# First pair of feed-forward slabs by plain block products, and layer norms on VectorE, in a hybrid encoder layer

## The chip, the core and the metric

The kernel runs on one core of a Trainium2 chip. The metric is the device time of one execution in microseconds (us). The engines are named as in the profile: PE (TensorE, with PEld for its weight loads), DVE (VectorE), ACT (ScalarE), POOL (GpSimd) and SP (SyncE, which issues the DMAs).

## The reference, cut to what matters

One layer of an encoder with 1024 tokens of width 1024 in float32. Four layer norms end four sublayers; the first and third are half-step feed-forward layers with 2816 hidden columns:

```python
x = layer_norm(ALPHA * x + 0.5 * swiglu(x, ffn1_w1, ffn1_w3, ffn1_w2), ln1_g, ln1_b)
...                                   # attention and state-space mixers, w_out
x = layer_norm(ALPHA * x + merged @ w_out, ln2_g, ln2_b)
x = layer_norm(ALPHA * x + 0.5 * swiglu(x, ffn2_w1, ffn2_w3, ffn2_w2), ln3_g, ln3_b)
ple = sigmoid(x @ ple_w_gate) * (p @ ple_w_proj)
x = layer_norm(ALPHA * x + ple, ln4_g, ln4_b)

def swiglu(x, w1, w3, w2):
    return (silu(x @ w1) * (x @ w3)) @ w2
def layer_norm(x, g, b):              # over the 1024 columns
    return (x - mean) * rsqrt(var + 1e-5) * g + b
```

## The kernel before, in words

Every float32 factor is split into a high part that TensorE takes as it is and a low rest (`split`, L64 on ACT for the high part, L65 on DVE for the low one), and a product is three matmuls: high by high, high by low, low by high. A matmul has a 128x128 stationary block and 512 moving columns.

**The upward half of a feed-forward layer** (`ffn_up`) goes through 11 pairs of 128-column slabs of w1 and w3 (`NP` is 11; slab p goes with slab p + 11). For a pair, x and the two slabs are cut into two-by-two blocks (halves of the 1024 model rows, halves of the tokens for x, the two slabs for w), and the four block results come from 7 block products by a Strassen-Winograd scheme instead of 8. One block product is 12 matmuls (`prod`, L246), so a pair is 2 x 7 x 12 = 168 matmuls for w1 and w3. The seven factors of x (numbers 1 to 7 in `blocks_of`: xa holds 1 and 2, tb 6 and 5, tc 7 and 3, td 4) are made once: 1, 2 and 3 are blocks of x as they are, 4 to 7 need differences of blocks. The seven factors of w are made for each slab pair by `sums_of`. `product` adds up the block products in PSUM and SBUF, and after a pair four further combinations c1 and c2 of the result are made on POOL (L330 to L333) and written with the rest to `hd` in DRAM (L336), for the downward half (`ffn_down`, L405), which uses the same scheme.

**The first pair.** In the first layer x comes already transposed from DRAM (`rawx`, L482, four pairs of rows for each half of the tokens). `lead` loads the first slabs of w1 and w3, splits the first token half, runs block products 1 and 2 for both slabs (48 matmuls, L502), and then makes the differences of x: L511 and L513 on DVE, L520 and L521 on POOL, each followed by splits. The remaining 120 matmuls of the pair need the differences. In the second layer x comes from the second norm and is transposed by TensorE (`transpose_sums`, L170): token tiles 0 to 3 give factors 1 and 2, and for each of the tiles 4 to 7 the function turns tile j - 4 once more, copies it (L184), turns tile j, and makes all differences (L187, L188, L192 on DVE, L193 on POOL). `lead2` starts block products 1 and 2 and then calls `finish()`, which does tiles 4 to 7.

**A norm** (`layer_norm`, L118 to L140) of one tile of 128 tokens: the mean on DVE, the sum of squares on ACT (L121), eight operations on 128x1 columns, mostly on DVE (L122 to L128, L137), the square root on ACT (L123), then the tile itself: scaled and shifted on ACT (L138), times the gain on POOL (L139), plus the bias on DVE (L140). The last two tiles of the last norm take another way, two pairs of DVE operations on half a tile (L132, L134). The norms run as their tiles leave the matrix product before (`norm_in`): after a few tiles (`lag`) each step also transposes an earlier tile for the next product. In norms one, two and three the next product cannot start before tiles are normalised, transposed (L151, L170) and split.

**Order.** The program is written as a flow of tiles; a scheduler puts the instructions of each engine into one queue at compile time, by program order as priority and by a simulated time line. An engine works through its queue in that order. A tag with `bufs` is a set of buffers; a tile waits for one to come free. The tag "raw" (weight slabs before the split) has four, "uh" and "ul" (split slabs) three, "v" four, "a" eight, the PSUM tags "up" two and "dn" four.

Of the kernel before, what the change touches and what calls it, by code (L numbers as in the profile page):

```python
# [20 lines left out]
F32 = mybir.dt.float32  # L21
# [24 lines left out]
def layer_kernel(ctx, tc, A):  # L46
# [66 lines left out]
    def layer_norm(a, sums, gt, bt, pool, out=None):  # L113
# [15 lines left out]
        if out is not None:  # L129
            cs = [slice(c, c + 512) for c in (0, 512)]  # L130
            for c in cs:
                V.scalar_tensor_tensor(out=a[:, c], in0=a[:, c], scalar=nm, in1=gt[:, c], op0=ALU.add, op1=ALU.mult)  # L132
            for c in cs:
                V.scalar_tensor_tensor(out=a[:, c], in0=a[:, c], scalar=rs, in1=bt[:, c], op0=ALU.mult, op1=ALU.add)  # L134
                nc.sync.dma_start(out[:, c], a[:, c])
            return
# [25 lines left out]
    def transpose_sums(a, j, X, pool):  # L162

        (xa, tb, tc_, td), c = X, j % 4
        cs = slice(c * 128, c * 128 + 128)

        def turned(src):
            t = pup.tile([128, 1024], F32, tag="up", name="tln")
            for k in range(8):
                PE.transpose(t[:, k * 128:k * 128 + 128], src[:, k * 128:k * 128 + 128], idt)  # L170
            return t

        def k8(t):
            return t.rearrange("p (k n) -> p k n", n=128)

        if j < 4:
            t = turned(a[j])
            split(k8(t), xa[0][:, :, cs], xa[1][:, :, cs])
            return
        l, r = slice(0, 512), slice(512, 1024)  # L180
        t1 = turned(a[j - 4])
        pool = pool[0]
        o = pool.tile([128, 1024], F32, tag="v", bufs=4, name="xo")
        S.activation(o, t1, AF.Copy)  # L184
        t2 = turned(a[j])
        p = pool.tile([128, 1024], F32, tag="v", bufs=4, name="xp")
        V.tensor_tensor(out=p[:, r], in0=t2[:, l], in1=o[:, l], op=ALU.subtract)  # L187
        V.tensor_tensor(out=p[:, l], in0=t2[:, r], in1=p[:, r], op=ALU.subtract)  # L188
        split(k8(p), tb[0][:, :, cs], tb[1][:, :, cs])
        q = pool.tile([128, 1024], F32, tag="v", bufs=4, name="xq")  # L190
        S.activation(q[:, r], t2[:, r], AF.Copy)
        V.tensor_tensor(out=q[:, l], in0=q[:, r], in1=t2[:, l], op=ALU.subtract)  # L192
        G.tensor_tensor(out=o[:, l], in0=o[:, r], in1=p[:, l], op=ALU.subtract)  # L193
        split(k8(q), tc_[0][:, :, cs], tc_[1][:, :, cs])
        split(k8(o[:, l]), td[:, 0:4, cs], td[:, 4:8, cs])

    def norm_in(steps, acc, gt, bt, xT, pool, done=None, lag=3, sums_in=None):


        ready = []  # L200

        def bring(late):
            j = ready.pop(0)
            if sums_in:
                transpose_sums(acc, j, xT, sums_in)
            else:
                transpose_in(acc[j], j, xT, late)
            if done:
                done(j)

        def finish():
            while ready:
                bring(True)

        for j, sums in steps:
            layer_norm(acc[j], sums, gt, bt, pool)
            ready.append(j)
            if len(ready) > lag:
                bring(False)
        return finish  # L220
# [53 lines left out]
    def ffn_up(fp, X, w1, w3, hd, lead):  # L274
# [5 lines left out]

        def product(A, B, left, right, d21, begun=None):

            x, z = begun or start(A, B)
# [23 lines left out]
        for p in range(NP):  # L307
            begun = None, None
            if p == 0:
                rest, begun = lead(banks, start)  # L310
                A1 = rest[0]()
            else:
                A1 = sums_of(fp, *slabs_in(w1, p))
            s1, s2 = big("s1"), big("s2")
            product(A1, X, s1, s2, lambda x: S.activation(s2[:, l], x, AF.Silu), begun[0])
            S.activation(s1, s1, AF.Silu)
            S.activation(s2[:, r], s2[:, r], AF.Silu)
            A3 = rest[1]() if p == 0 else sums_of(fp, *slabs_in(w3, p))
# [5 lines left out]
            product(A3, X, e1, e2, times, begun[1])  # L324
# [3 lines left out]

            c1, c2 = big("c1"), big("c2")
            G.tensor_tensor(out=c1[:, l], in0=s1[:, r], in1=s2[:, r], op=ALU.add)  # L330
            G.tensor_tensor(out=c1[:, r], in0=c1[:, l], in1=s1[:, l], op=ALU.subtract)
            G.tensor_tensor(out=c2[:, l], in0=s1[:, l], in1=s1[:, r], op=ALU.subtract)
            G.tensor_tensor(out=c2[:, r], in0=s2[:, l], in1=c1[:, r], op=ALU.subtract)  # L333
            for i, t in ((1, s1[:, l]), (2, s2[:, l]), (4, s2[:, r]), (5, c1[:, l]), (6, c1[:, r]),
                         (7, c2[:, l]), (3, c2[:, r])):
                nc.sync.dma_start(hd[i - 1][p // 2][:, p % 2, :], t)  # L336
# [121 lines left out]
    with tc.tile_pool(name="f1", bufs=1, reuse_waits="tile") as fp:  # L458
# [6 lines left out]
        def lead(banks, start):  # L465
# [27 lines left out]
            B = blocks_of(xa, tb, tcs, td)  # L493
            bk = [banks() for _ in range(2)]
            for i, (x, y) in ((1, (0, 512)), (2, (512, 1024))):
                n = 0
                for k in range(4):
                    ks = slice(x + k * 128, x + k * 128 + 128)
                    for (o1, o2), (_, (wh, wl), _) in zip(bk, ws):
                        o = o1 if i == 1 else o2  # L500
                        for m, (u, v) in enumerate(((wh, 0), (wh, 1), (wl, 0))):
                            PE.matmul(o, lhsT=u[:, ks], rhs=B[i][v][:, k, :], start=(k == 0 and m == 0),  # L502
                                      stop=(k == 3 and m == 2), skip_group_check=True)
            for kp in range(2):
                bring(1, kp), bring(1, kp + 2)
            r2 = [load_raw(A[n][NP]) for n in ("ffn1_w1", "ffn1_w3")]
            t2s = []
            for kp in range(2):
                k = 2 * kp
                t1, b21, b12, b22 = raws[0][kp], raws[0][kp + 2], raws[1][kp], raws[1][kp + 2]  # L510
                V.tensor_tensor(out=t1, in0=b12, in1=t1, op=ALU.subtract)  # L511
                t2 = fp.tile([128, 2, 512], F32, tag="v", bufs=4, name="t2")
                V.tensor_tensor(out=t2, in0=b22, in1=t1, op=ALU.subtract)  # L513
                split(t2, tb[0][:, k:k + 2, :], tb[1][:, k:k + 2, :])
                t2s.append(t2)
            for kp in range(2):
                k = 2 * kp
                t1, b21, b12, b22 = raws[0][kp], raws[0][kp + 2], raws[1][kp], raws[1][kp + 2]
                split(t1, tb[0][:, k + 4:k + 6, :], tb[1][:, k + 4:k + 6, :])
# [897 lines left out]
```

## Time and profile before

| what | value |
|---|---|
| median of 3 runs | 2406.77 us (2405.56 to 2407.76) |
| the profiled execution's own time | 2407.14 us |
| its span in the profile | 2405.3 us |
| PE, DVE, ACT, POOL busy | 2273.2, 1625.7, 984.0, 623.6 us |
| granted clock of TensorE, mean | 0.974 |

The span runs from the first to the last instruction in the trace; the execution's own time is 1.8 us longer. In the timelines below a row gives the start in us, the duration in us, the engine, the line, the operation, its tiles and, in brackets, how long the engine had stood idle before it and what ended that.

### The profile page before, as it was taken

To read this page: it belongs to the slowest core of one execution; us is meant where nothing else is said; L and a number is where in the kernel's file an instruction comes from. 1 tells how busy PE (TensorE), PEld (TensorE's weight loads), DVE (VectorE), ACT (ScalarE), POOL (GpSimd) and SP (SyncE) were. 2 spreads that over 40 slices of the span, in tenths; PEclk is the share of its full clock that TensorE was granted. 3 is DMA by queue.
4 is the path that set the end of the run, shared out by engine and by line. 5 is a ranking of instruction groups with operands and counts; after the bars stand their busy time and mean duration, and the time that the engine had idled before them with its cause. 6 is when DMAs were issued, how large, how long until landed. Compare 5 with 4: busy or idle time off the path is not lost.

```text
span 2405.3 us, 28500 instructions
## 1 busy us (share of the span) xinstructions
PE 2273.2 (95%) x10704; PEld 1867.9 (78%) x10704; DVE 1625.7 (68%) x2316; ACT 984.0 (41%) x1390; POOL 623.6 (26%) x545
## 2 busy tenths in 40 slices
PE   5999999999979989998999999969999999999898
PEld 4888888877768878886888888758888888777686
DVE  7656565775587799948688875675656556764845
ACT  4333333333442313334477871353333333333627
POOL 2111010200038555524255542220201112000302
PEclk8999999999989989999999999979999999999899
DMA  3333232842244223335100034112323236622211
GB/s 122 113 97 120 84 114 86 316 184 95 81 143 144 94 75 90 105 127 214 62 10 27 27 129 160 40 57 93 122 88 119 88 110 255 239 94 95 75 53 70
DMA packets 103898, 265.62 MB, mean 110 GB/s; under 512 B 13264, under 2 KB 27856, under 8 KB 103760
## 3 DMA queue, kind: packets, MB, share of 16 engines
q1 hardware_dynamic: 103760, 263.80, 32.1%
q8 instruction: 84, 1.38, 0.2%
q14 instruction: 54, 0.44, 0.1%
HBM read 189.33 MB, written 74.42 MB: 110 GB/s over the span
## 4 chain that ended last, share of the span: by engine, by line
PE 76%; DVE 10%; issue 5%; DMA 4%; ACT 2%; POOL 1%; SPq 0%; DVEq 0%; ACTq 0%; POOLq 0%
PE px L246 19%; PE pg L84 11%; PE py L246 10%; PE pdy L405 7%; PE pd L405 7%; PE pz L246 5%; PE ps L84 3%; PE pd L84 2%; PE pov L693 2%; PE pya L84 2%; PE tpp L680 2%; DMA w2w<-in_ffn_w_dram 2%; PE pyb L84 2%; PE pq L84 1%; DVE acc L140 1%
## 5 line engine op out<-in xcount | busy, mean ns | idle before, releaser
L139 POOL TENSOR_TENSOR acc<-acc,ln 128x1024 f32<-128x1024 f32 x30 | 79.5, 2656 | 555.6 <-ACT acc L138 554.2
L330 POOL TENSOR_TENSOR c<-s,s 128x512 f32<-128x512 f32 x22 | 30.2, 1375 | 725.7 <-DVE s L325 654.4
L65 DVE TENSOR_TENSOR wlo<-raw,whi 128x1024 fp32r<-128x1024 f32 (+4 forms) x112 | 141.6, 1268 | 80.2 <-ACT whi L64 79.0
L64 ACT ACTIVATE whi<-raw 128x1024 fp32r<-128x1024 f32 (+4 forms) x112 | 107.6, 967 | 154.9 <-PE pg L84 111.7
L84 PE MATMUL pg<-xlo,whi 128*128 128x512 f32 x416 | 164.7, 396 | 0.3 <-DVE xlo L65 0.3
L84 PE MATMUL pg<-xhi,whi 128*128 128x512 f32 x416 | 164.8, 397 | 0.1
L84 PE MATMUL pg<-xhi,wlo 128*128 128x512 f32 x416 | 163.6, 393 | 0.0
L405 PE MATMUL pd<-wl,hh 128*128 128x512 f32 x352 | 144.0, 409 | 5.9 <-DVE wl L65 5.9
L405 PE MATMUL pd<-wh,hl 128*128 128x512 f32 x352 | 140.6, 403 | 0.0
L405 PE MATMUL pd<-wh,hh 128*128 128x512 f32 x352 | 125.3, 405 | 10.5 <-ACT hh L64 5.3
L64 ACT ACTIVATE wh<-w2w 128x1024 fp32r<-128x1024 f32 x56 | 59.3, 1058 | 166.3 <-PE pd L405 84.0
L246 PE MATMUL py<-tch,fhl 128*128 128x512 f32 x352 | 116.9, 392 | 0.0
L64 ACT ACTIVATE fhl<-raw 128x512 fp32r<-128x512 f32 x44 | 27.9, 633 | 202.3 <-PE px L246 197.2
L246 PE MATMUL px<-td,thi 128*128 128x512 f32 x352 | 108.8, 390 | 0.0
L65 DVE TENSOR_TENSOR hl<-raw,hh 128x1024 fp32r<-128x1024 f32 x84 | 101.3, 1208 | 10.2 <-ACT hh L64 8.2
L667 POOL TENSOR_SCALAR P<-P,sm 128x1024 f32<-128x1024 f32 x64 | 74.7, 1168 | 115.0 <-DVE sm L666 97.2
L260 DVE TENSOR_TENSOR c<-raw 128x512 f32<-128x512 f32 x44 | 37.8, 859 | 98.4 <-PE px L246 98.4
L405 PE MATMUL pdy<-wl,hh 128*128 128x512 f32 x264 | 104.3, 395 | 0.0
L405 PE MATMUL pdy<-wh,hl 128*128 128x512 f32 x264 | 103.9, 395 | 0.0
L405 PE MATMUL pdy<-wh,hh 128*128 128x512 f32 x264 | 99.7, 395 | 0.0
L65 DVE TENSOR_TENSOR wl<-w2w,wh 128x1024 fp32r<-128x1024 f32 x56 | 69.4, 1239 | 36.6 <-ACT wh L64 36.4
L65 DVE TENSOR_TENSOR pt<-tpp,pt 128x512 fp32r<-128x512 f32 x128 | 85.6, 684 | 11.6 <-ACT pt L64 10.1
(413 smaller groups left out, 6667.1 us busy)
## 6 DMA issues: line engine op xcount, KB each, us to landing
raw<-in_ffn_w_dram SPq DMA_DIRECT2D x86, 512.0 KB, 3.7
raw<-hd SPq DMA_DIRECT2D x70, 512.0 KB, 3.3
hd<-c SPq DMA_DIRECT2D x88, 256.0 KB, 4.4
hd<-s SPq DMA_DIRECT2D x66, 256.0 KB, 2.9
w2w<-in_ffn_w_dram SPq DMA_DIRECT2D x32, 512.0 KB, 8.7
rawx<-in_xT_dram SPq DMA_DIRECT2D x16, 256.0 KB, 5.2
w2e<-in_ffn_w_dram SPq DMA_DIRECT2D x8, 512.0 KB, 8.9
acc<-in_x_dram SPq DMA_DIRECT2D x8, 512.0 KB, 9.1
```

The source lines that it names most:

```text
L64: S.activation(hi, src, AF.Copy)
L65: V.tensor_tensor(out=lo, in0=src, in1=hi.bitcast(F32), op=ALU.subtract)
L84: PE.matmul(out, lhsT=a, rhs=b, start=(n == 0), stop=(n == last))
L139: G.tensor_tensor(out=a, in0=a, in1=gt, op=ALU.mult)
L140: V.tensor_tensor(out=a, in0=a, in1=bt, op=ALU.add)
L246: PE.matmul(out, lhsT=x[:, ks], rhs=y[:, k, :], start=(first and n == 0), stop=(n == 11), skip_group_check=True)
L260: V.tensor_tensor(out=c[:, r], in0=r2[:, l], in1=r2[:, r], op=ALU.add)
L330: G.tensor_tensor(out=c1[:, l], in0=s1[:, r], in1=s2[:, r], op=ALU.add)
L405: PE.matmul(P[t], lhsT=x[:, ts], rhs=y[:, ws], start=(fresh and p + a == 0 and m == 0), stop=(p + a == NP - 1 and m == 2), skip_group_chec ...
L667: G.tensor_scalar(out=P, in0=P, scalar1=sm, scalar2=1.0, op0=ALU.mult, op1=ALU.mult)
L680: PE.transpose(tp[:, k * 128:k * 128 + 128], P[:, (q * 4 + k) * 128:(q * 4 + k) * 128 + 128], idt)
L693: PE.matmul(p[:, 0:256], lhsT=vt[:, k, c0:c0 + 128], rhs=pt[k // 4][b][:, k % 4, :], start=(k == 0 and b == 0), stop=(k == 7 and b == 1))
```

## The change

The first pair of slabs of each feed-forward layer is computed by 8 plain block products for each of w1 and w3 in place of 7 (`plain`, 192 matmuls instead of 168), in four runs of 48: first token half with row 0 (slab 0) and row 1 (slab 11), then second half with row 1 and row 0. The second half takes what stands in the places of factors 4 and 3 (td and the second half of tc): the two plain blocks of x of that token half; td gets its factor 4 only afterwards. The differences of x are made in place on DVE (`differences`) and split after the first two runs have been put into the queue; the last factor (td) is written in `ends`, after the next pair's first two block products are issued. In the second layer the differences are made on the tiles before they are turned, so that each tile of 4 x 128 columns is turned again. The first pair's results stand in two "raw" buffers. c1 and c2 are made on DVE for all pairs (`finish`). All norms take the way with two DVE operations, on whole tiles except for the last two.

```diff
-        V.tensor_tensor(out=nm, in0=nm, in1=rs, op=ALU.mult)
-        S.activation(a, a, AF.Identity, bias=nm, scale=rs)
-        G.tensor_tensor(out=a, in0=a, in1=gt, op=ALU.mult)
-        V.tensor_tensor(out=a, in0=a, in1=bt, op=ALU.add)
+        cs = [slice(0, 1024)] if out is None else [slice(c, c + 512) for c in (0, 512)]
+        for c in cs:
+            V.scalar_tensor_tensor(out=a[:, c], in0=a[:, c], scalar=nm, in1=gt[:, c], op0=ALU.add, op1=ALU.mult)
+        for c in cs:
+            V.scalar_tensor_tensor(out=a[:, c], in0=a[:, c], scalar=rs, in1=bt[:, c], op0=ALU.mult, op1=ALU.add)
...
-    def transpose_sums(a, j, X, pool):
+    def transpose_blocks(a, j, X):
+        (xa, _, tc_, td), c = X, j % 4
+        cs = slice(c * 128, c * 128 + 128)
+        t = turned((a[j][:, 0:512], a[j][:, 512:1024]))
         if j < 4:
+            split(t, xa[0][:, :, cs], xa[1][:, :, cs])
             return
+        split(t[:, 0:4, :], td[:, 0:4, cs], td[:, 4:8, cs])
+        split(t[:, 4:8, :], tc_[0][:, 4:8, cs], tc_[1][:, 4:8, cs])
+
+    def differences(b11, b21, b12, b22):
+        V.tensor_tensor(out=b22, in0=b22, in1=b12, op=ALU.subtract)
+        V.tensor_tensor(out=b12, in0=b12, in1=b11, op=ALU.subtract)
+        V.tensor_tensor(out=b11, in0=b22, in1=b11, op=ALU.add)
+        V.tensor_tensor(out=b21, in0=b21, in1=b11, op=ALU.subtract)
...
+    def plain(B, ws, half, row, s):
+        u, g = [pdn.tile([128, 512], F32, tag="dn", name=n) for n in ("pu", "pg")]
+        for i, b in enumerate(((B[1], B[2]), (B[4], B[3]))[half]):
+            for k in range(4):
...
+                            PE.matmul(o, lhsT=x[:, ks], rhs=b[y][:, k, :], ...)
+            yield
+        S.activation(s, u, AF.Silu)
+        V.scalar_tensor_tensor(out=s, in0=s, scalar=0.5, in1=g, op0=ALU.mult, op1=ALU.mult)
...
+        s0, ends = first()
+        for p in range(1, NP):
+            A1 = sums_of(fp, *slabs_in(w1, p))
+            begun = start(A1, X)
+            if p == 1:
+                ends()
+                finish(0, *s0)
...
-            G.tensor_tensor(out=c1[:, l], in0=s1[:, r], in1=s2[:, r], op=ALU.add)
+            V.tensor_tensor(out=c1[:, l], in0=s1[:, r], in1=s2[:, r], op=ALU.add)
...
+            for row, s in ((0, s1), (1, s2)):          # first layer
+                for _ in plain(X1, w, 0, row, s[:, l]):
+                    pass
             for kp in range(2):
+                differences(raws[0][kp], raws[0][kp + 2], raws[1][kp], raws[1][kp + 2])
...
+            for row, s in ((1, s2), (0, s1)):
+                last.append(plain(X1, w, 1, row, s[:, r]))
+                next(last[-1]), next(last[-1])
...
+        for row, s in ((0, s1), (1, s2)):              # second layer
+            for _ in plain(X2b, w, 0, row, s[:, l]):
+                pass
         finish()
...
+        for row, s in ((1, s2), (0, s1)):
+            last.append(plain(X2b, w, 1, row, s[:, r]))
+            for _ in range(2):
+                next(last[-1])
+                differences(acc[c][:, l], acc[c][:, r], acc[c + 4][:, l], acc[c + 4][:, r])
+                t = turned((acc[c][:, l], acc[c + 4][:, l]))
+                split(t, tb[0][:, :, cs[c]], tb[1][:, :, cs[c]])
+                c += 1
...
+        for c in (0, 2):
+            t = turned((acc[c + 4][:, r], acc[c + 5][:, r]))
...
+        def ends():
...
+            for c in (0, 2):
+                t = turned((acc[c][:, r], acc[c + 1][:, r]))
```

In both layers the second slab of row 1 (w3) is split into two "v" buffers, and the slabs of row 1 are loaded before the second half of x.

## Rows read from the trace of the kernel before

**Rows 1.** The page, busy us and share of the span by engine.
```profile
PE 2273.2 (95%) x10704; PEld 1867.9 (78%) x10704; DVE 1625.7 (68%) x2316; ACT 984.0 (41%) x1390; POOL 623.6 (26%) x545
```
**Rows 2.** Waits of PE, whole span: us in total, times, longest us.
```profile
PE px L246 <- ACT shi L64: 23.6, 2, 17.9
PE tln L151 <- DVE acc L140: 15.1, 2, 11.8
PE tln L170 <- ACT xo L184: 10.4, 3, 4.0
```
**Rows 3.** Windows of PE: us, busy us (matmuls), granted clock, DMA share, GB/s.
```profile
5.40:19.70 14.30, 13.81 (x48) 1.00 0.98 375
19.70:37.50 17.80, 0.00 (x0) 0.60 0.00 1
37.50:71.70 34.20, 31.04 (x121) 0.86 0.19 62
71.70:110.40 38.70, 38.70 (x170) 1.00 0.33 109
...
1618.10:1651.60 33.50, 31.97 (x124) 0.86 0.20 63
```
**Rows 4.** Timeline of the first layer's start, POOL and DVE.
```profile
15.66 3.44 POOL L520 TENSOR_TENSOR rawx<-rawx 128x1024 f32<-128x1024 f32 x1 [14.37 <-DVE rawx L511]
...
16.75 3.43 DVE L65 TENSOR_TENSOR tbl<-rawx,tbh 128x1024 fp32r<-128x1024 f32 x1
...
23.41 1.21 DVE L65 TENSOR_TENSOR tbl<-t,tbh 128x1024 fp32r<-128x1024 f32 x1
```
**Rows 5.** Timelines of DVE, POOL and PE after the first norm.
```profile
691.14 0.15 DVE L137 TENSOR_TENSOR ln<-ln,ln 128x1 f32<-128x1 f32 x1
...
695.23 3.09 POOL L139 TENSOR_TENSOR acc<-acc,ln 128x1024 f32<-128x1024 f32 x1 [15.42 <-ACT acc L138]
...
699.88 3.30 DVE L140 TENSOR_TENSOR acc<-acc,ln 128x1024 f32<-128x1024 f32 x1
...
703.33 1.94 PE L151 MATMUL tln<-idt,acc 128*128 128x128 f32 x8 [11.78 <-DVE acc L140]
```
**Rows 6.** Timeline of PE at the second layer's start.
```profile
1577.76 0.80 PE L246 MATMUL px<-xah,whi 128*128 128x512 f32 x1 [0.96 <-ACT xah L64]
...
1591.27 1.91 PE L170 MATMUL tln<-idt,acc 128*128 128x128 f32 x16
...
1603.69 3.56 PE L170 MATMUL tln<-idt,acc 128*128 128x128 f32 x16 [3.97 <-ACT xo L184]
```
**Rows 7.** Groups of DVE, 1538 to 1578: busy us, mean ns, then idle before.
```profile
L126 DVE TENSOR_TENSOR ln<-ln,ln 128x1 f32<-128x1 f32 x6 | 4.8, 802 | 0.0
L125 DVE TENSOR_TENSOR ln<-ln 128x1 f32<-128x1 f32 x6 | 4.5, 745 | 0.0
```
**Rows 8.** Waits of PE, 2225 to 2315.
```profile
PE pgate L84 <- DVE wlo L65: 4.7, 2, 3.2
PE tln L151 <- DVE acc L140: 3.3, 1, 3.3
```
**Rows 9.** Groups of DVE, 2262 to 2292.
```profile
L65 DVE TENSOR_TENSOR wlo<-raw,whi 128x1024 fp32r<-128x1024 f32 x4 | 7.0, 1744 | 0.0
...
L128 DVE TENSOR_TENSOR ln<-ln,ln 128x1 f32<-128x1 f32 x4 | 2.8, 701 | 0.0
```
**Rows 10.** Line L325, whole span: duration in ns, least, median, most.
```profile
L325 DVE SCALAR_TENSOR_TENSOR s<-s,e x22: 1216/1218/1222, 76.3 to 2032.8; 128x1024 f32<-128x1024 f32 x22
```
**Rows 11.** Tile acc on DVE from 2335 on: duration in ns, least, median, most.
```profile
L140 DVE TENSOR_TENSOR acc<-acc,ln x6: 1212/1224/1225, 2356.3 to 2391.6; 128x1024 f32<-128x1024 f32 x6
L132 DVE SCALAR_TENSOR_TENSOR acc<-acc,ln,ln x4: 740/744/1154, 2390.5 to 2399.1; 128x512 f32<-128x512 f32 x4
```
**Rows 12.** Timeline of DVE and POOL at the end of a later pair.
```profile
308.15 1.83 DVE L260 TENSOR_TENSOR c<-raw 128x512 f32<-128x512 f32 x1
...
309.38 1.75 POOL L331 TENSOR_TENSOR c<-c,s 128x512 f32<-128x512 f32 x1
```

More of the change, by code (lines that the diff above doesn't have):

```diff
@@ L184, in transpose_sums @@
[L184 to L192, printed above, removed]
@@ L492, in lead @@
                     part(slice(256, 1024))
[L493 to L503, printed above, removed]
+            more = [wload(A["ffn1_w1"][NP])]
@@ new lines, in first1 @@
+            r2 = load_raw(A["ffn1_w3"][NP])
+            for kp in range(4):
+                bring(1, kp)
+            more.append([fp.tile([128, 1024], F32R, tag="v", bufs=4, name=n) for n in ("whi", "wlo")])
+            split(r2, *more[1])
+            w = [(a[1], b) for a, b in zip(ws, more)]
+            s1, s2 = load_raw_tile(), load_raw_tile()
+            l, r = slice(0, 512), slice(512, 1024)
+            for kp, (hi, lo) in enumerate(((td[:, 0:2], td[:, 4:6]), (td[:, 2:4], td[:, 6:8]),
+                                           (tcs[0][:, 4:6], tcs[1][:, 4:6]), (tcs[0][:, 6:8], tcs[1][:, 6:8]))):
+                split(raws[1][kp], hi, lo)
@@ L922, in layer_kernel, with first2, ends @@
-    ffn_up(fp, blocks_of(*X2), A["ffn2_w1"], A["ffn2_w3"], hd, lead2)
+    X2b = blocks_of(*X2)
+    def first2():
+        l, r = slice(0, 512), slice(512, 1024)
+        w = [[None, None], [None, None]]
+        for row, i, name in ((0, 0, "ffn2_w1"), (0, 1, "ffn2_w3"), (1, 0, "ffn2_w1"), (1, 1, "ffn2_w3")):
+            if row and i:
+                hl = [fp.tile([128, 1024], F32R, tag="v", bufs=4, name=n) for n in ("whi", "wlo")]
+                split(load_raw(A[name][NP]), *hl)
+            else:
+                hl = wload(A[name][row * NP])
+            w[i][row] = hl
+        s1, s2 = [wts.tile([128, 1024], F32, tag="raw", bufs=RAW, name="raw") for _ in range(2)]
+        for row, s in ((0, s1), (1, s2)):
+            for _ in plain(X2b, w, 0, row, s[:, l]):
+                pass
+        finish()
+        cs = [slice(c * 128, c * 128 + 128) for c in range(4)]
+        c, last = 0, []
+        for row, s in ((1, s2), (0, s1)):
[6 more added lines that the diff above has]
+                c += 1
+            if row:
+                for _ in last[0]:
+                    pass
+        tch, tcl = X2[2]
+        for c in (0, 2):
+            t = turned((acc[c + 4][:, r], acc[c + 5][:, r]))
+            for i in range(2):
+                split(t[:, 4 * i:4 * i + 4], tch[:, 0:4, cs[c + i]], tcl[:, 0:4, cs[c + i]])
+        def ends():
+            for _ in last[1]:
+                pass
+            td = X2[3]
+            for c in (0, 2):
+                t = turned((acc[c][:, r], acc[c + 1][:, r]))
+                for i in range(2):
+                    split(t[:, 4 * i:4 * i + 4], td[:, 0:4, cs[c + i]], td[:, 4:8, cs[c + i]])
+        return (s1, s2), ends
```

129 lines of the change are left out of this document (48 added, 81 removed).

## The prediction, made before the change was run

> **What bounds the kernel now.** I read the busy shares first: PE is busy for 95% of the span and DVE for 68% [rows 1]. So time is to be had where PE stands still, or from fewer matmuls; the change adds matmuls (24 for each feed-forward layer), so all its gain must come from standing time. The second view is who PE waited for [rows 2]: the longest entries are the first shi of a pair (23.6 us in two waits, the longest 17.9), the normalised tile before its transposition (15.1) and the copy of the first transposition in the second layer (10.4). All three lie where the change works: the start of the two feed-forward layers and the norms. The third view cuts out the first start [rows 3]: 48 matmuls run until 19.7, none until 37.5, then 120 that fill the time to 71.7; from there on a pair of 168 (the view counts 170 with those on the edges) takes 38.7 us, 0.2304 us for each matmul, with PE full and the clock at 1.00. In the second start the same 120 take until about 1651 [rows 3]. Last, why the waits are so long: a DVE subtraction of 128x1024 takes 1.21 us alone and 3.43 us beside a POOL operation [rows 4], and after the first norm the bias takes 3.30 us beside a POOL gain of 3.09 [rows 5]. POOL thus costs its own time and stretches DVE, which is the engine that everybody waits for there.
>
> **The first layer's start.** Before, the 168 matmuls are through at about 71.6. The change puts 192 in, with work for PE from the first run on. The first 48 are the same and depend on the same loads, so they end at 19.7. The other 144 cost 144 x 0.2304 = 33.2 us if nothing stops them: 52.9. The cover: while 33 us of matmuls run, DVE must split the row-1 slabs and the second half of x (6 operations of 1.21), make 8 differences and 6 splits (14 of 1.21), evict two or three times (0.74 each at most) and make the factors of the next w1 (about 6 us): some 32 us, spread well, since each part is needed one run of 11 us after the other. So it just fits, and with no POOL beside it each costs 1.21. SP has two slabs more to issue ahead of the second half of x; the transfers there ran at 375 GB/s [rows 3], so 1 MB delays that half by about 3 us, and its split is needed only at 31. The new wait: the next pair needs new "uh" and "ul" buffers, two of which are held until the last run ends; a split into high and low then stands between, 0 to 2.4 us (two operations of about 1.21). I take 1.8 and get 18.8 - 1.8 = 17 saved. The two "raw" buffers held by the first pair's results also delay the loads of the next w3 slabs; these are needed only 84 matmuls (19 us) after the next pair starts, and eviction, combinations and stores take about 12 us, so I cost it at nothing; without that cover each us late is one lost.
>
> **A norm.** Out go ACT L138, POOL L139 and DVE L140 (1.22) and L137 (0.15); in come two DVE operations of 128x1024 with three operands. The trace has none with a column scalar at that size. Its half-size form takes 0.744 [rows 11], so twice that, 1.49, is the upper end; the full-size form with a constant takes 1.218 [rows 10], the lower end. I take 1.3, near the second, since it has the same shape. DVE then has 2 x 1.3 - 1.22 - 0.15 = 1.23 more for each norm, and loses the stretch by POOL of some 2.1 (3.30 against 1.21). The first of the two can run during the square root, so that only one stands after the scalars.
>
> The Vector Engine (DVE) Microarchitecture Reference of the Trainium skill (section 7, points that are easy to get wrong) says that this kind of operation runs at half its rate with two float32 inputs in SBUF. The trace does not agree: line L325 is such an operation and takes 1.218, no more than the two-operand L140 of the same shape at 1.22 [rows 10, 11]; by the rule it would be about 2.4, and it is a rival below.
>
> **The first norm.** From the last scalar at 691.1 to the biased tile at 703.2 it takes 12.0 us, and PE stands 11.8 [rows 5]. After: the first DVE operation, the second, and two weight splits of 1.22 that stood in between, 5 us at most, 1.3 at least. So PE goes on at 694 to 697: 6 to 9 saved, 8 taken. Before that, four tiles overlap the last products; there DVE gets 4 x 1.23 more and loses four stretches of about 2.1, 3.5 us net, of which I count 1. Sum 9. What follows starts with loads and small operations that wait for the same transposes, so it all moves along.
>
> **Second norm and second layer's start.** DVE is what decides when factors 1 and 2 are ready, at 1577.8 [rows 6]. Up to there its stretched column operations lose (0.802 - 0.15) x 6 + (0.745 - 0.15) x 6 = 7.5 us [rows 7], and five L140 cost 6.1; in their place come five times 2.6, 13.0. So this point does not move; I take 1577. Then 96 matmuls: the first 48 took 13.5 us there, 2.4 of it at the lower clock, so 22.1 + 2.4 = 24.5, to 1602. Then the four second-half tiles are turned and split with two PSUM buffers, about 7 us of which PE works four: 1609. The norms of these tiles, which had cost standing time, lie under the 96 matmuls. Then 96 matmuls and four turnings (8 transposes take 0.95, by 1.91 for 16 [rows 6]): 22.1 + 3.8, to 1635; the differences (4 of at most 0.74 for a tile) lie beside them. Two turnings with a wait for a buffer, 3 us: 1638; two more inside the next pair, 2: 1640, against 1651 before. 11 saved. DVE has nearly as much to do in this stretch as it is long, so the ends are 3 and 17. The differences also wait for the stores of x2 (SP, on the same queue as the slabs), which land before 1609.
>
> **Third and fourth norm.** After the third norm PE waits 4.7 for weight splits and 3.3 for a tile [rows 8]; DVE's stretches there are (0.701 - 0.15) x 4 = 2.2 for each of three column lines, of which one is shown, and (1.744 - 1.21) x 4 = 2.1 [rows 9], 8.7 in all against 4 x 1.23 = 4.9 more. With the shorter way from the scalars to the tile I take 5 (2 to 9). The fourth norm is hidden by the matmuls; at the very end one of the half-size operations no longer is stretched to 1.154 [rows 11]: 1 at most, taken.
>
> **c1 and c2 on DVE.** 22 pairs x 4 operations of at most 0.74, 3.0 a pair. Beside POOL three DVE operations of a pair took 1.8 in place of 0.7 [rows 12], 3.3 that go. DVE's net is about nothing, and PE is full through these stretches [rows 3]; 0. The last pair's stores could go out 3 us earlier before each downward half; from -5 to 0, taken 0.
>
> **Sum.** 17 + 9 + 11 + 5 + 1 = 43; 2407.1 - 43 = 2364. The profiled execution lies 0.4 us above the median of 2406.8, which changes nothing.
>
> **Rivals.**
> 1. *The norms become bound by DVE and the second start gains little* (one engine instead of two does the norm's work). For it: [rows 7], by which that stage's DVE work does not shrink. Then only the first start and a part of the first norm are left, 17 + 4 = 21: 2386. The band from 2378 to 2399 belongs to it. 0.22.
> 2. *Slower: the stretch is not POOL's.* If DVE's long operations come from something else (PSUM or DMA traffic), the 24 norms ahead of a product cost 1.23 each plus the stretch that stays on two operations instead of one, some 2.1: 24 x 3.3 = 79, at least 0.6 of it on PE's path, 48, and the second start gains nothing. Against 17 of the first start: 2407 + 31 = 2438; it turns slower once a norm costs over 0.7 net. Against it: every long DVE row that I looked at lies under a POOL row, and those beside none have 1.21 [rows 4, 5, 12]. 0.04.
> 3. *A three-operand operation on two float32 tiles takes twice its time.* 48 such in the three norms ahead of a product cost 1.2 more each, 58, which takes the 43 away and adds 15: 2422. Against it speak [rows 10]. This is the rule of the Trainium skill named above. 0.02.
> 4. *The change does not do what it says*: the scheduler's queues put the differences or the next weights so late that PE stands as long as before. It would be 2403 to 2411. For it: order comes from a simulated time line. Against: four runs of matmuls are there to fill. 0.04.
>
> **Numbers.** A measurement of this kernel can tell about 0.2%, 4.8 us. The forecast (2346 to 2378, a gain of 29 to 61) has 0.68; rivals 0.22, 0.04, 0.02, 0.04. Faster is 0.68 + 0.22 = 0.90; same 0.04; slower 0.06. The range that leaves 0.2 out takes the forecast's own bounds (first start 15 to 19, first norm 7 to 11, second start 3 to 17, third norm 2 to 9) and most of the first rival: 2346 to 2390.
>
> **What would show it.** Right: matmuls without a gap from 5.4 to about 53 in the first start and the next pair from there; PE's wait after the first norm at 3 us in place of 11.8; no DVE operation of 128x1024 above 1.5 outside the state-space and attention stages; the 96 matmuls of the second start from about 1550 (its time shifted by 26) and 11 us less to the next pair; PE full in later pairs. Wrong: a wait of PE on DVE in the second start, on slo or differences, of over 5 us (rival 1); long DVE operations with POOL idle (rival 2); the norms' new operations at 2.4 or more (rival 3); a wait of the next pair's w3 on its load.

## The result, and the profile after

The changed kernel takes 2373.99 us (median of 4 runs, 2369.38 to 2375.43) where the kernel before, in the same session, takes 2406.16: a ratio of 0.9865, 95% interval 0.9848 to 0.9882. That is 32 us less, against 43 forecast; the time lies inside the range and inside the forecast's own band, 4 us from its slower end. The rest of this section goes through the profiled execution (span 2373.6 us, where the one before had 2405.3), in the order of the groups ahead of the prediction.

The page, busy time and share by engine, to be read against [rows 1]: PE has 80 instructions more (48 matmuls and 32 transposes), POOL lost 233 us, and DVE is not busier although it took over POOL's work.

```profile
PE 2280.4 (96%) x10784; PEld 1876.8 (79%) x10784; DVE 1586.0 (67%) x2388; ACT 938.4 (40%) x1344; POOL 390.2 (16%) x419
```

Waits of PE over the whole span (us in total, times, longest), the answer to [rows 2]. The three entries of before are gone or changed: no wait for shi or xo is left, but one of 10.4 stands where the 11.8 after the first norm stood.

```profile
PE tln L146 <- DVE ln L128: 10.4, 1, 10.4
PE pu L270 <- ACT xah L64: 7.2, 2, 6.0
PE pd L412 <- ACT hh L64: 6.6, 2, 3.8
...
PE tln L162 <- DVE tcl L65: 4.1, 2, 3.6
```

**The first layer's start.** Windows of PE (us, busy us and matmuls, granted clock, DMA share, GB/s), the answer to [rows 3]: the 17.8 us without a matmul are full, and so is everything to the end of the first later pair.

```profile
6.00:20.00 14.00, 13.65 (x49) 1.00 0.96 370
20.00:37.50 17.50, 17.50 (x77) 1.00 0.29 92
37.50:53.00 15.50, 15.50 (x69) 1.00 0.17 56
53.00:92.00 39.00, 39.00 (x170) 1.00 0.30 100
```

Groups of DVE from 5 to 55 us (busy us, mean ns, idle before), the answer to [rows 4]: no operation of 128x1024 is stretched any more, and the differences cost what was counted.

```profile
L65 DVE TENSOR_TENSOR tbl<-rawx,tbh 128x1024 fp32r<-128x1024 f32 x4 | 4.8, 1219 | 0.0
...
L178 DVE TENSOR_TENSOR rawx<-rawx 128x1024 f32<-128x1024 f32 x2 | 2.4, 1222 | 0.0
```

**The first norm.** Timeline of DVE around and behind the end of the last matmul of the downward half (672.44), the answer to [rows 5]. Nothing is stretched, and yet PE stands 10.35 us: DVE is busy for all of it (a window from 672.44 to 682.79 has DVE at 10.35 of 10.35). What PE waits for is the operation at 681.37. Ahead of it in DVE's queue stand the first operations (L131) of this tile and the three others, 1.28 each, and the two weight splits; between them lie the split of a turned tile, an eviction and column operations.

```profile
671.15 1.28 DVE L131 SCALAR_TENSOR_TENSOR acc<-acc,ln,ln 128x1024 f32<-128x1024 f32 x1
672.35 1.22 DVE L65 TENSOR_TENSOR xlo<-tln,xhi 128x1024 fp32r<-128x1024 f32 x1
...
674.15 1.28 DVE L131 SCALAR_TENSOR_TENSOR acc<-acc,ln,ln 128x1024 f32<-128x1024 f32 x1
...
675.53 1.28 DVE L131 SCALAR_TENSOR_TENSOR acc<-acc,ln,ln 128x1024 f32<-128x1024 f32 x1
...
676.79 2.34 DVE L65 TENSOR_TENSOR wlo<-raw,whi 128x1024 fp32r<-128x1024 f32 x2
...
679.24 1.28 DVE L131 SCALAR_TENSOR_TENSOR acc<-acc,ln,ln 128x1024 f32<-128x1024 f32 x1
...
681.37 1.28 DVE L133 SCALAR_TENSOR_TENSOR acc<-acc,ln,ln 128x1024 f32<-128x1024 f32 x1
```

The timeline of PE at the same place has one row:

```profile
682.79 1.94 PE L146 MATMUL tln<-idt,acc 128*128 128x128 f32 x8 [10.35 <-DVE ln L128]
```

**The second layer's start.** Waits of PE from 1540 to 1640, the answer to [rows 6]; together they are 7.4 us.

```profile
PE tln L162 <- DVE tcl L65: 4.1, 2, 3.6
PE pu L270 <- ACT xah L64: 1.2, 1, 1.2
PE pu L270 <- DVE ln L127: 0.8, 1, 0.8
PE pu L270 <- ACT td L64: 0.7, 1, 0.7
PE pu L270 <- DVE td L65: 0.6, 1, 0.6
```

The norm's two operations there, groups of DVE from 1520 to 1640, stand where [rows 7] had column operations of 0.75 to 0.80:

```profile
L131 DVE SCALAR_TENSOR_TENSOR acc<-acc,ln,ln 128x1024 f32<-128x1024 f32 x8 | 10.2, 1274 | 0.0
L133 DVE SCALAR_TENSOR_TENSOR acc<-acc,ln,ln 128x1024 f32<-128x1024 f32 x8 | 10.0, 1276 | 0.0
```

**The third norm.** Waits of PE from 2200 to 2260, the answer to [rows 8]: 4.7 and 3.3 have become 2.3, 2.0 and 1.1.

```profile
PE pgate L84 <- DVE wlo L65: 2.3, 2, 1.5
PE pgate L84 <- ACT whi L64: 2.0, 1, 2.0
...
PE tln L146 <- DVE ln L127: 1.1, 1, 1.1
```

**Where the 31.7 us of the span lie**, by the time at which PE reaches the same instruction in both traces. The first matmul comes 0.55 later. The first matmul of the first downward half moves from 453.53 to 435.31, so the upward half gives 18.8. From there to the state-space stage (first pw, 821.96 to 800.17) 3.6 are added. In the stages behind it, to the last pya (1538.23 to 1521.58), 5.1 are lost, in code that the change does not touch. PE has the same 3847 matmuls in the same order there; 1.1 of the 5.1 are pauses, 4.1 are matmuls that ran longer. To the second downward half (2027.40 to 1999.38) 11.4 are added, and to PE's end (2393.94 to 2360.91) 5.0. The last output then lands 4.2 us after DVE's last operation instead of 3.1: a loss of 1.3 between PE's end and the span's.

### The profile page after: what moved, and what is told of

Its sections match the earlier page's. It is cut to its first block, busy times and chain, and to the rows that moved or that the text cites. A ratio compares the mean times of both kernels' runs of the same rounds, so it can differ in the third digit from the quotient of the medians.

```text
span 2373.6 us, 28494 instructions
## 1 busy us (share of the span) xinstructions
PE 2280.4 (96%) x10784; PEld 1876.8 (79%) x10784; DVE 1586.0 (67%) x2388; ACT 938.4 (40%) x1344; POOL 390.2 (16%) x419
## 3 DMA queue, kind: packets, MB, share of 16 engines
q1 hardware_dynamic: 103760, 263.80, 32.3%
## 4 chain that ended last, share of the span: by engine, by line
PE 83%; DVE 7%; DMA 4%; issue 2%; ACT 2%; POOL 1%; SPq 0%; DVEq 0%; ACTq 0%; POOLq 0%
PE px L232 18%; PE pg L84 11%; PE py L232 9%; PE pdy L412 8%; PE pd L412 7%; PE pz L232 5%; PE pd L84 3%; PE pgate L84 3%; PE ps L84 3%; PE pov L706 2%; PE pu L270 2%; PE pg L270 2%; PE tpp L693 2%; PE pya L84 2%; DMA w2w<-in_ffn_w_dram 2%
## 5 line engine op out<-in xcount | busy, mean ns | idle before, releaser
L232 PE MATMUL py<-tch,fhl 128*128 128x512 f32 x320 | 106.0, 392 | 0.0
L65 DVE TENSOR_TENSOR hl<-raw,hh 128x1024 fp32r<-128x1024 f32 x84 | 94.9, 1132 | 11.3 <-ACT hh L64 11.2
L232 PE MATMUL px<-td,thi 128*128 128x512 f32 x320 | 98.8, 390 | 0.0
L84 PEld LDWEIGHTS pg<-xhi,whi 128*128 128x128 f32 x416 | 78.5, 189 | 17.2 <-issue 1.0
L84 PEld LDWEIGHTS pg<-xlo,whi 128*128 128x128 f32 x416 | 78.6, 189 | 16.8 <-DVE xlo L65 0.8
```

Source lines behind the costliest of these rows:

```text
L65: V.tensor_tensor(out=lo, in0=src, in1=hi.bitcast(F32), op=ALU.subtract)
L84: PE.matmul(out, lhsT=a, rhs=b, start=(n == 0), stop=(n == last))
L232: PE.matmul(out, lhsT=x[:, ks], rhs=y[:, k, :], start=(first and n == 0), stop=(n == 11), skip_group_check=True)
```

## The experiments

In the table, idle is the sum of PE's pauses of over 0.1 us in the profiled execution. Slow is what matmuls of 512 columns took beyond 0.2304 us each, where the next one followed without a pause 0.25 to 0.7 us later, so the price of the lower of TensorE's two clock levels (1.2 GHz; a granted clock of 1.00 is 2.4) for these matmuls. Idle and slow thus belong to one execution, the time and the ratio to all runs of a kernel. The ratio is that to the kernel before in the same session, whose medians were 2406.2, 2406.7, 2407.8 and 2403.6 us. The last of these sessions (c1, c2 alone; norms, c1, c2; pairs, c1, c2; last pair's c1, c2 on POOL) ran on another chip than the two before it (that of the first is not on record); the kernel before takes some 3 us less there, so these four compare with the others by the ratio.

| kernel | us | ratio, 95% interval | idle | slow |
|---|---|---|---|---|
| before | 2406.2 | 1 | 114.7 | 39.5 |
| norms alone | 2388.95 | 0.9929, 0.9916 to 0.9941 | 105.5 | 31.6 |
| pairs alone | 2379.08 | 0.9887, 0.9871 to 0.9902 | 83.2 | 31.0 |
| c1, c2 alone | 2408.62 | 1.0017, 1.0008 to 1.0026 | 114.0 | 38.6 |
| norms, c1, c2 | 2389.03 | 0.9932, 0.9918 to 0.9945 | 106.7 | 32.3 |
| pairs, c1, c2 | 2385.58 | 0.9910, 0.9894 to 0.9926 | 83.9 | 34.5 |
| pairs and norms | 2361.85 | 0.9820, 0.9804 to 0.9835 | 71.9 | 24.9 |
| all three: the change | 2373.99 | 0.9865, 0.9848 to 0.9882 | 74.2 | 32.8 |
| the change, fifth tile turned later | 2362.67 | 0.9824, 0.9809 to 0.9839 | 68.7 | 28.4 |
| the change, start shifted once | 2368.89 | 0.9843, 0.9828 to 0.9858 | 73.1 | 30.7 |
| the change, start shifted twice | 2374.22 | 0.9865, 0.9848 to 0.9881 | 73.8 | 29.9 |
| the change, last pair's c1, c2 on POOL | 2368.85 | 0.9849, 0.9835 to 0.9864 | 74.4 | 28.8 |
| pairs and norms, start shifted once | 2365.58 | 0.9829, 0.9809 to 0.9848 | 69.7 | 25.4 |
| pairs and norms, fifth tile later | 2362.60 | 0.9814, 0.9799 to 0.9828 | 67.5 | 29.0 |

### Norms alone, and pairs alone

The first takes the kernel before and gives it the new norm:

```
-        V.tensor_tensor(out=nm, in0=nm, in1=rs, op=ALU.mult)
-        S.activation(a, a, AF.Identity, bias=nm, scale=rs)
-        G.tensor_tensor(out=a, in0=a, in1=gt, op=ALU.mult)
-        V.tensor_tensor(out=a, in0=a, in1=bt, op=ALU.add)
...
+            V.scalar_tensor_tensor(out=a[:, c], in0=a[:, c], scalar=nm, in1=gt[:, c], op0=ALU.add, op1=ALU.mult)
...
+            V.scalar_tensor_tensor(out=a[:, c], in0=a[:, c], scalar=rs, in1=bt[:, c], op0=ALU.mult, op1=ALU.add)
```

> The kernel before with the new norm alone (two three-operand DVE operations in place of the ACT, POOL and DVE ones); first pairs and c1, c2 as before. Theory A, POOL's stretch of DVE was on PE's path at all three norms that a product follows: first norm 4 gained (what the changed kernel shows there), way to the second start 5, second start with the old sums 2 to 6, third norm 5, in all 16 to 20: 2386 to 2390 us, ratio 0.992 to 0.993. Rival B, the first pairs alone made the gain, and the norms' new DVE work eats what the stretch gives back: 2403 to 2408, ratio 0.999 to 1.001.

Measured: 2388.95 us, as theory A has it. The second takes the changed kernel, puts the same lines of the norm back and c1, c2 on POOL.

> The changed kernel with the old norm (ACT, POOL, DVE) and with c1, c2 back on POOL: the plain first pairs alone. Theory A, the first layer's start gives 17 to 18 whatever the norm does, and the second start, with the old norms under its 96 matmuls, 4 to 8: 2381 to 2385 us, ratio 0.989 to 0.991. Rival B: 2372 to 2376, ratio 0.986 to 0.988, as the changed kernel. Rival C, the second start needs the short norm (its four late tiles are stretched by POOL to over 3 us each and the 96 matmuls run out before): only the first start is left, 2387 to 2391, ratio 0.992 to 0.994.

Measured: 2379.08 us, 2 better than theory A's band and away from B and C. By the ratios the norms give 0.71% and the pairs 1.13%, and both together (next experiment) 1.80%: they add up, to about 43 us, which is the sum that the prediction had for them.

The second layer tells them less apart. From the last pya to the first pgate the kernel before takes 728.1 us, norms alone 714.8, pairs alone 719.8, both 709.7, and the change 714.6; this stretch takes in the third norm. Up to the point where PE first runs out of matmuls in the second downward half, the norms alone gain 9.4 us, the pairs alone 5.3, both 12.1 and the change 11.8. So at the second start the norms by themselves bring 9 of the 12. Waits of PE there with the norms alone (1550 to 1640) show what they leave to the pair: the old sums' copy and shi still hold PE 17 us, which the pair turns into work, but it pays for that with 24 matmuls (5.5 us) and 32 transposes.

```profile
PE tln L165 <- ACT xo L179: 11.6, 3, 5.3
PE px L241 <- ACT shi L64: 5.7, 1, 5.7
```

### c1 and c2 back on POOL

```
-            V.tensor_tensor(out=c1[:, l], in0=s1[:, r], in1=s2[:, r], op=ALU.add)
+            G.tensor_tensor(out=c1[:, l], in0=s1[:, r], in1=s2[:, r], op=ALU.add)
...
```

> The changed kernel with c1 and c2 of all 22 pairs back on POOL. My term for them was 0, because PE is full in the pairs: 2371 to 2377 us, ratio 0.986 to 0.988, and the pairs keep their 38.7 us. Rival: POOL's stretch of DVE in the pairs delays factors or evictions, or the last pair's stores delay the downward half: 2379 to 2384, ratio 0.989 to 0.991.

Measured: 2361.85 us, 12 less than the change, while my theory had no difference and the rival had the wrong sign. The intervals of the two ratios do not touch, so the kernel with the third part of the change is the slower one. But the two traces differ in places where nothing differs in the code: from the first downward half to the end of attention PE has the same 5347 matmuls in the same order, and on the other engines, but for the last pair's c1, c2 at its beginning, single neighbours change places. Both kernels start that stretch level (435.31 and 435.46), and the one with c1, c2 on POOL is 9 us faster at its end (it reaches the last pya at 1512.70, the change at 1521.58). From the state-space stage on it is 7.3 us faster, 2.1 of it in pauses and 5.2 in matmuls that ran shorter. The mean granted clock of the whole run is the first hint. The view by core of the change (span and clock):

```profile
core 0: 2373.6 us, clock 0.982
```

The same view with c1, c2 on POOL:

```profile
core 0: 2358.9 us, clock 0.987
```

### The fifth tile of the first norm turned later

```
-        finish = norm_in(chain([first], dn), acc, *ln, x1T, fp, spill)
+        finish = norm_in(chain([first], dn), acc, *ln, x1T, fp, spill, 4)
```

The 4 is the `lag` of the norm, which is 3 elsewhere.

> The changed kernel with the fifth tile of the first norm turned behind the first half of the next products instead of ahead of it. Theory A, the 10.35 us that PE waits after the first norm come from the order of the queues: the fifth tile's second operation stands on DVE behind the other tiles' first operations and two weight splits, and the products wait behind its transposition on PE. Then the products start once the weights are split, 4 to 6 us earlier: 2368 to 2370 us, ratio 0.984 to 0.985, and the longest wait there is under 7. Rival B, DVE as a whole is the bound there: the wait moves behind the first half of the products, where the four late tiles come as late as before, and the time stays at 2372 to 2376, ratio 0.986 to 0.988.

Measured: 2362.67 us, 11 less, twice what theory A gave, and not for its reason. Counted from the last matmul of the downward half, the products do start 6.7 us earlier (5.2 us behind it, at 671.45, instead of 11.9, at 684.38). The wait breaks into 4.34 and 2.30 us, but then 14 matmuls run at the lower clock, and the transpositions of the late tiles end about as late as before (26.4 us behind that matmul instead of 27.0). From the last matmul of the downward half to the state-space stage the change takes 127.7 us and this kernel 127.1: the edit itself gave under 1 us there. The rest of the 11 came from stretches with the same queues but for single neighbours. The clearest: near the end of the first downward half both kernels have the same wait, with one pause of 0.5 us and no other in the 30 us before it, and then the same matmuls. The wait in the change, timeline of PE:

```profile
643.82 0.50 PE L412 MATMUL pd<-wl,hh 128*128 128x512 f32 x1 [1.99 <-DVE wl L65]
```

The 4.4 us behind it in the change, windows of PE (us, busy us and matmuls, granted clock, DMA share, GB/s):

```profile
643.82:648.22 4.40, 4.40 (x13) 0.64 0.46 141
```

The same wait in the kernel with the tile turned later, timeline of PE:

```profile
640.02 0.50 PE L412 MATMUL pd<-wl,hh 128*128 128x512 f32 x1 [1.99 <-DVE wl L65]
```

And the 4.4 us behind it there, windows of PE:

```profile
640.02:644.42 4.40, 4.40 (x19) 1.00 0.47 138
```

A wait of 1.99 us is followed by 4.4 us at a mean granted clock of 0.64 (19 matmuls become 13) in one kernel, and by full speed in the other. In the first downward half as a whole the slow matmuls cost 5.4 us in the change and 1.1 here. It is not the chip: behind the same wait (1.97 us) the kernel of pairs and norms, run in one session and on one chip with this one, loses 1.7 us to slow matmuls in the 12 us that follow (granted clock 0.61 in the first 4.4 of them), and this one 0.1.

### The start shifted

The first slab's first 256 columns are loaded once more, or twice more, ahead of everything; behind the first layer's start the order on the engines is the same but for single neighbours that change places.

```
-            part(slice(0, 256))
+            nc.sync.dma_start(ws[0][0][:, 0:256], ws[0][2][:, 0:256]); part(slice(0, 256))
```

> The changed kernel with its first slab's first 256 columns loaded twice, so that everything behind starts one small transfer (some 2 us) later, with the order on the engines else the same. Theory C, what the clock costs after each wait of PE depends on when the wait falls and not on what the change did: waits of the same 2 to 3 us in the downward halves cost 0 in one kernel and up to 2.9 us in another, and the matmuls that ran slowly add up to 32.8 us in the changed kernel against 24.9 with c1 and c2 on POOL. Then the time moves by several us for a shift of 2, to 2362 to 2372 us (ratio 0.982 to 0.986), with the slow matmuls at 24 to 30 us. Theory D, the changed kernel's loss is its own (c1 and c2 on DVE): 2374 to 2378, ratio 0.987 to 0.988, slow matmuls at 31 to 34.

> As before, with the columns loaded three times (some 4 us later). Theory C: again another time, anywhere from 2362 to 2378 us, the sum of the slow matmuls and not the sum of the waits telling most of the difference. Theory D: 2375 to 2380.

> c1 and c2 on POOL with the start shifted once. Theory C: 2362 to 2374 us, not the 2362 of the unshifted one but for chance. Theory D, the gain is that of the edit: 2361 to 2366.

Measured: the first matmul comes 1.0 and 5.5 us later than in the change, and the time is 2368.89 and 2374.22, so behind the start both are some 5 to 6 us faster than the change, which is about as much as the intervals of the ratios leave open. Slow is 30.7 and 29.9 where the change has 32.8, above theory C's band in the first. With c1, c2 on POOL the shift costs 3.7 us for a start 1.5 later, and 2365.58 lies in the bands of both theories. Theory D misses the first two, the second by under 1 us. That the clock takes or gives a few us (theory C) is shown better by the runs of a single kernel: with c1, c2 on POOL and the shift, two took 2361.46 and 2361.98 us at a mean granted clock of 0.987, and two 2369.19 and 2369.80 at 0.983 and 0.984. Whether the shift itself did anything cannot be told from that scatter. The order of the two families stays here: with c1, c2 on POOL 2361.85 and 2365.58, with them on DVE 2373.99, 2368.89 and 2374.22. At the same shift the medians differ by 3.3 us, with some 6 either way by the intervals, so that theory D's 12 lies outside, though not by much; the two profiled executions lie 10.6 apart.

### Both edits

> c1 and c2 on POOL and the fifth tile of the first norm turned later, both edits together. By C, c1 and c2 give nothing and the later turning 4 to 6 us of waits, the rest is the clock's: 2360 to 2370 us, ratio 0.981 to 0.985. By D the gains add, 12 + 11: 2350 to 2354, ratio 0.977 to 0.979.

Measured: 2362.60 us. The gains of 12 and 11 do not add, as theory C has it. In the profiled executions the pauses do nearly add: against the change they are 2.4 us less with c1, c2 on POOL, 5.5 less with the later turning and 6.8 less with both. What does not add is the time of the matmuls themselves, all 10784 of them without the pauses: 10.7 us less, 6.2 less, and with both 5.7 less. This kernel, the kernel of pairs and norms and the one with the later turning alone lie within 1 us of each other and are the fastest of the study; they beat the change by some 0.5%. With the later turning, c1 and c2 on POOL no longer make a kernel faster.

### What c1 and c2 on DVE cost

Three kernels more complete the eight combinations, and one puts the last pair of each layer alone on POOL:

```
+            c1, c2, E = big("c1"), big("c2"), G if p == NP - 1 else V
...
```

> The kernel before with c1 and c2 of all pairs on DVE and nothing else. So far: norms alone take 17.7 us, pairs alone 27.6, and both without the move of c1 and c2 44.8, so these two add up and my sum of 43 was right but for the term of c1 and c2, which I had at 0 and which the changed kernel shows at 12; but with the start shifted it shows at 3, and with the later turning at 0. Theory E, the move has a price of its own, at the start of the downward halves (the last pair's stores come later, and SP's loads of the same data behind them): 2 to 4 us slower than before, 2408 to 2411, ratio 1.001 to 1.002, and the first wait of each downward half longer than the 2.55 and 2.73 us of before. Theory C, the 12 us are the clock's, by where the waits fall: within 3 us of before on either side with unchanged waits.

> Norms alone with c1 and c2 on DVE added. Theory E: 2 to 4 us above the 2389 of the norms alone, 2391 to 2393, ratio 0.993 to 0.995. Theory D: 12 above, 2401, ratio 0.998. Theory C: 2385 to 2397, by the slow matmuls.

> The plain pairs with the old norm, c1 and c2 on DVE: the changed kernel with the old norm alone. Theory E: 2 to 4 us above the 2379 of the pairs alone, 2381 to 2383, ratio 0.989 to 0.990. Theory D: 12 above, 2391, ratio 0.993. Theory C: 2375 to 2387, by the slow matmuls.

> The changed kernel with c1 and c2 of the last pair of each layer alone on POOL; PE's order is the same. Theory E: PE's waits before the downward halves fall from 2.85 and 3.79 us to about 2.1 and 1.5, some 3 us of waits, and the clock gives back up to 3 more: 2366 to 2371 us, ratio 0.983 to 0.985. Theory C: those waits go too, but the time goes where the clock goes, 2362 to 2376. Theory D, all pairs' operations cost: 2372 to 2374.

Measured: by the ratios the move of c1, c2 costs 4.1 us on the kernel before, 0.7 with the norms, 5.5 with the pairs, 10.8 with both, 3.4 with both and the start shifted, 2.4 with the fifth tile later. None of the six is a gain; the mean is 4.5, with some 2 either way by the intervals. By themselves the first and the fourth stand clear of the measurement, the third only just. Neither theory's bands hold for all: the norms lose less than E had, the pairs more, and on the kernel before the waits grew, which C had unchanged. Of theory E's mechanism the longer wait is seen in all six: the first waits of the two downward halves, together, grow by 1.1, 0.5, 1.4, 3.1, 1.9 and 2.2 us, 1.7 in the mean. Some of it comes back in shorter pauses later: all pauses of the two downward halves together grow by 0.0, 0.2, 1.4, 2.3, 1.2 and 1.4 us, 1.1 in the mean. Slow grows by 2.6 in the mean (from -0.9 to 7.8). These are single executions, whose spans differ by -0.2, 1.9, 5.0, 14.8, 10.6 and 0.7 us and not as the medians do; the first three pairs compare executions of different sessions as well, the second and third of different chips. Waits of PE from 2010 to 2070, early in the second downward half, in the change:

```profile
PE pd L412 <- ACT hh L64: 3.8, 1, 3.8
```

The same view with c1, c2 on POOL:

```profile
PE pd L412 <- ACT hh L64: 1.4, 1, 1.4
```

Behind this stands SP's queue, on which the last stores of c1, c2 and the loads of raw for the downward half follow each other. Timeline of SP in the change, where these loads go out 4.5 us before PE runs out of matmuls (2032.91):

```profile
2026.53 0.33 SPq L320 DMA_DIRECT2D hd<-c  x1
...
2028.42 3.44 SPq L69 DMA_DIRECT2D raw<-hd  x4
```

Timeline of SP with c1, c2 on POOL, where they go out 7.1 us before (2023.75):

```profile
2014.13 0.33 SPq L320 DMA_DIRECT2D hd<-c  x1
...
2016.68 2.80 SPq L69 DMA_DIRECT2D raw<-hd  x4
```

With the last pair alone on POOL the waits fell by 1.3 us (to 2.75 and 2.60), not the 3 expected, and slow by 4: 2368.85 us, inside E's band but with less of E's mechanism in it. In its first downward half the loads go out as early as with all pairs on POOL (6.05 us before PE runs out, against 6.13), but the first takes 8.1 us to land instead of 7.6; in the second they go out 5.6 us before, against 7.1. So the longer wait is not the last pair's alone; what the other pairs add was not tried. This kernel has the change's own order of matmuls over the whole program, and shows the clock once more: the pauses are 74.4 us here and 74.2 in the change, and the same 10784 matmuls take 2274.3 us here and 2280.3 in the change (the chip is another one here, and its part in this is not known). One place of it lies in the stage before attention. Timeline of PE in the change, with the waits:

```profile
1121.78 0.70 PE L84 MATMUL ps<-k,qh 96*128 96x512 f32 x2 [1.91 <-DVE gb L842]
1124.89 0.80 PE L84 MATMUL pyb<-sh,whi 128*128 128x512 f32 x1 [1.18 <-DVE gb L842]
```

The 5.11 us from the second of these rows, windows of PE in the change:

```profile
1124.89:1130.00 5.11, 5.11 (x12) 0.52 0.38 141
```

The same two rows, timeline of PE with the last pair on POOL:

```profile
1118.12 0.70 PE L84 MATMUL ps<-k,qh 96*128 96x512 f32 x2 [1.36 <-DVE gb L842]
1121.24 0.50 PE L84 MATMUL pyb<-sh,whi 128*128 128x512 f32 x1 [1.50 <-DVE gb L842]
```

And the 5.11 us there, windows of PE:

```profile
1121.23:1126.34 5.11, 4.32 (x17) 1.00 0.39 141
```

Twelve matmuls and seventeen in the same time (a few records can be missing), after waits that add up to 3.09 and 2.86 us.

## Why the prediction was right, and where not

**The first layer's start, 17: right.** It gave 18.8; the 1.8 us put aside for the next pair's buffers did not come, since PE has no pause of over 0.3 us from 12 to 468 us.

**The norm's operations: right.** 1.28 us each against 1.3 taken. The rule of the Trainium skill (Vector Engine (DVE) Microarchitecture Reference, section 7), by which they would run at half rate, does not hold here: 1.28 is 5% over the two-operand 1.22 of [rows 11]. Rivals 2 and 3 fall with these rows: without POOL no stretch is left. All 18 DVE operations of 128x1024 that still take over 1.5 us (1.5 to 3.4, from 746 to 1525) lie beside a POOL operation.

**The first norm, 9: the step that was mis-sized.** "The first DVE operation, the second, and two weight splits of 1.22 that stood in between, 5 us at most" left out that the first operations of all four late tiles come ahead of the second of the first one: the other three take 3.6 us, and a split, an eviction and column operations between them, which it did not count either, some 3 more. PE's wait only went from 11.8 to 10.35, and the whole stretch gave 3.6, not 9. What the shorter norm saved in stretch it gave back in queue. Turning the tile later moves the wait rather than ends it.

**Second start, 11, and third norm, 5: the sizes right (11.4 and 5.0), the split of the second not.** I had the way to factors 1 and 2 unmoved and all 11 behind it. In the traces 5.8 came ahead of it (px at 1577.76 against pu at 1555.34, a shift of 22.4 after 16.7), and the norms alone bring 9 us up to the second downward half without the plain pair. Rival 1 was out: its "norms become bound by DVE" is true of the first norm only.

**c1 and c2, 0: wrong, and on the other side of its bounds.** "The last pair's stores could go out 3 us earlier before each downward half; from -5 to 0" read the move as relief for the stores. The runs show the reverse: the first waits of the downward halves grow by 1.7 us, and the time by 4.5 in the mean over six pairs of kernels. PE being full in the pairs was right (the change and the kernel with c1, c2 on POOL reach the first downward half at 435.31 and 435.46). In the measured change the difference is 10.8 us, and it is what parts 32 from the 43 forecast: the kernel without it gains 1.80% of 2406, 43 us. Most of it is not shown to be the edit's own: of the 14.8 us between these two profiled executions 10.7 are matmuls that ran longer, 2.4 are pauses and the rest lies at the two ends. That the other terms come to 43 is luck in part. In the trace of pairs and norms the first norm's stretch gave 5.3 us in place of 9, while the second layer, from the last pya to PE's end, gave 21 in place of 16, and the stages between gave 2 where nothing was forecast.

**The stages that I did not look at, 0: 5.1 lost.** The change loses 5 us between the state-space stage and the last pya, with the same instructions. From the state-space stage to the last pya the kernels of this study take either 714.1 to 717.0 us, as the one before (716.3), or 719.6 to 721.4, as the change (721.4), with the same matmuls in the same order but for single neighbours: pairs alone, pairs with c1, c2, c1, c2 alone and the start shifted once lose there as well, the others do not. I had taken a stage without an edit as a stage without a difference; 4.1 of the 5.1 us are matmuls that ran longer, and behind waits of 1 to 2 us in it the clock falls in one kernel and not in another.

**The tail, 1: -1.3.** DVE's last operation came 32.8 us earlier; the last output took 1.2 us longer to land. In the kernel with the fifth tile turned later, whose end is the same code, it lands 3.1 us behind DVE's last operation, as before, so the edit is not shown to be the reason.

What stays open: how much of the 10.8 us is c1 and c2 and how much the clock's chance; the six pairs give 0.7 to 10.8, 4.5 in the mean.

## What to carry to other kernels

Split a change of several parts before believing its sum: here two parts made the whole forecast gain, and with the third, counted at nothing because PE was full beside it, a quarter of it was gone. When an operation leaves a slow engine for a busy one, look at what is queued behind it and at the transfers that wait for its result, and count all the operations of a group that queue ahead of the one that is awaited. Between variants that differ by under 0.5%, compare the sum of PE's pauses and of its slow matmuls by stage before naming a cause.

## What the runs showed of the hardware

The same wait, with the same matmuls around it, is followed by the lower clock in one kernel and not in another: 1.99 us of wait, then 4.4 us at 0.64 or at 1.00; waits of 1.91 and 1.18 us, then 0.52, against 1.36 and 1.50 us, then 1.00. Over the kernels of the table the slow matmuls add up to 24.9 to 39.5 us, with 7.8 us of difference between the change and the kernel of pairs and norms. The runs of one kernel lie 3 to 9 us apart as well, and the granted clock goes with them (2361.46 and 2361.98 us at 0.987, 2369.19 and 2369.80 at 0.983 and 0.984, with pairs, norms and the shift). The Trainium skill (TensorE: Matmul & The Clock Gate, Part 1) says that the monitor behind the clock runs freely and does not start anew with the kernel, so that the place where the level changes varies; these rows agree, in that the place differs between kernels with the same matmuls in the same order. No run here shows what the monitor looks at.
